# Sixteen instead of thirteen units of half-products in the first FFN, with fewer buffers for the adaLN pieces

## The chip, the cores and the metric

The kernel runs on one core of a Trainium2 chip. The metric is the device time of one execution in microseconds (us). PE is TensorE (matmuls; PEld its weight loads), DVE VectorE, ACT ScalarE, POOL GpSimd, SP SyncE, which issues nearly all DMAs; SPq is its DMA queue.

## The reference, cut to what matters

A two-layer trunk over 512 tokens of width 1024 in float32: a gated convolution mixer, an FFN, an SSD mixer, an FFN, each between two RMS norms and with shift, scale and gate from a conditioning vector c.

```python
mod = (jax.nn.silu(c) @ ada_w + ada_b).reshape(bsz, DEPTH, 2, 3, D_MODEL)
...
def swiglu_ffn(h, w_in, w_out):
    gate, up = jnp.split(h @ w_in, 2, axis=-1)
    return (jax.nn.silu(gate) * up) @ w_out
```

The change touches the FFN of the first layer: `h` is 512 x 1024, `w_in` 1024 x 5632 (2816 gate and 2816 up columns, 22 features of 128 columns each), `w_out` 2816 x 1024. `ada_w` is 1024 x 12288.

## The kernel before

Every float32 operand is split into a high half (a cast on ACT) and a low half (a subtraction on DVE); a product takes three matmuls for each 128 rows: high x high, high x low, low x high.

**In-projection.** A *chunk* (`in_chunk`, L318) is one feature's gate or up: 24 matmuls of 128x512. A *unit* (`Units`, from L612) makes two features' gate (even u) or up (odd u) at once, by seven half-products P1 to P7 of 12 matmuls of 128x256 each, from sums and differences of the weight's and the tokens' quarters: 84 small matmuls where two chunks take 48 large ones. Features 0 to 3 are chunks; then 13 units make features 4 to 15 and the gates of 16 and 17, and ten chunks make what is left. `UN1` (L1304) is the number of units.

**A unit's parts.** Unit u issues the DMAs for unit u + 2 (`fetch`): on SP the two sum quarters `sg` (L632, L633), then into the stage `wsu` the quarter [8:12] (L635), the two quarters of X, 512 KB, (L637) and the quarter [12:16] (L639); POOL then adds with two accumulating DMAs (L1403). PE runs P1(u), P7(u-1), P5(u), P2(u), P4(u-1), P6(u), P3(u). ACT casts X for u + 1 (L656), keeps results from the matmul banks (L704), casts Z, Y, S (L647); DVE makes the low halves (L660 for X, L648 for the others), combines results (c12 L712, c22 L721, c11 L708) and forms the sums Y and S (`sum_y` L673, `sum_s` L677). The banks of PE are few: P4(u-1) writes the bank from which c22(u-1) reads; P7(u-1) that from which ACT keeps A's high half.

**adaLN sums.** c's product with `ada_w` is made beside the units. A piece of `ada_w` (128 x 1024, 512 KB) is loaded into a tile `ada_st` (`ada_load`, L1040, its DMA at L1044), a *madd* on DVE (L128; L126 for the first of eight) adds it to `ada_acc`, and after eight a fold (L141) and a small matmul follow, whose results become `mods` (L152). Three pieces are loaded ahead; each madd is followed by the next `ada_load`. `sums(n)` (L1392) runs n such steps; it stands behind c11 in the units, one step in each even unit and in every one after the sixth. The tiles come from a pool of three buffers (L795).

**Order.** All engines follow the order in which the code is written. An instruction on SP that waits for a buffer holds up every later one on SP. Behind the units, the out-projection runs 28 products in seven groups (`seq`) and some plain ones, with its weights loaded by `x_load`, `xy_load`, `y_load`, and splits made ahead (`w_prep`, `a_prep`). Features up to 15 keep their raw product in `raw`; later ones are split at once.

```python
            for u in range(UN1):
                if not end:
                    un.fetch(u + 2)
                un.product(u, "P1")
                un.high_x(u + 1)
...
                un.c11(u)
                if u and (u % 2 == 0 or u > 6):
                    sums(1)
                un.split_z(u)
```

Of the kernel before, what the change touches and what calls it, by code (L numbers as in the profile page):

```python
# [16 lines left out]
P = 128  # L17
# [21 lines left out]
def trunk_kernel(  # L39
# [572 lines left out]
    class Units:  # L612
# [4 lines left out]
        def __init__(self, w1, h, tq, sums_w, s_tile, raw_at, gates, raw_done, count):  # L617
            self.w1, self.h, self.tq, self.sums_w = w1, h, tq, sums_w
            self.s_tile, self.raw_at, self.gates, self.raw_done, self.count = s_tile, raw_at, gates, raw_done, count
            self.staged, self.wts, self.banks, self.outs = {}, {}, {}, {}  # L620
# [6 lines left out]
        def fetch(self, u):  # L627
# [10 lines left out]
            if u:  # L638
                dma(st[:, 12:16, :], self.cols(u - 1, 1, 1))  # L639
# [28 lines left out]
        def split_s(self, u):  # L668
            self.split("S", u, self.s_tile(u), self.staged[u][0][:, 4:8, :])

# [121 lines left out]
    with ExitStack() as ph:  # L792
        sums_p, first_p = ExitStack(), ExitStack()
        gx = ph.enter_context(tc.tile_pool(name="gx", bufs=1, side="right", reuse_waits="tile"))
        ada_p.append(sums_p.enter_context(tc.tile_pool(name="adap", bufs=3, side="right", reuse_waits="tile")))  # L795
# [13 lines left out]

        def xn_tile():  # L810
# [11 lines left out]
        xf2s = ([ada_p[0].tile([P, 2, T], F32, tag="ada", name="xf") for _ in range(3)]  # L822
# [80 lines left out]
        with tc.manual_schedule(engines={PE_ENGINE, mybir.EngineType.SP, mybir.EngineType.Activation,  # L903
# [132 lines left out]

            def ada_tile():
                return ada_p[0].tile([P, 2, 512], F32, tag="ada", name="ada_st")
# [265 lines left out]
        UN1 = 13  # L1304
# [56 lines left out]

        def raw_done(f):
            if f % 4 == 3:
# [123 lines left out]
        def behind(q):  # L1487

            for t in range(2):
# [8 lines left out]
                elif q == at["s", 6 * per - 1]:  # L1498
                    held[1, 2 + t] = c22[:, t, :]
                    act.activation(c22[:, t, :], bank["A", t], AF.Copy, scale=-1.0)  # L1500
# [8 lines left out]
        with tc.manual_schedule(engines={PE_ENGINE, mybir.EngineType.SP, mybir.EngineType.Activation,  # L1509
                                         mybir.EngineType.DVE, mybir.EngineType.Pool}):  # L1510
            part_of = Units(f_w_in[0], h, tq, sums_w, s_tile, lambda f: raw[f // 4][:, f % 4, :], gates,
                            raw_done, UN1)
# [49 lines left out]
            un, fu, pp = part_of, 3 + UN1, UN1 + 1  # L1562
            for u in range(UN1):
                v = u - 1
                end = u == UN1 - 1
                if not end:
                    un.fetch(u + 2)
                else:
                    more_n = load_w([(f_w_in[0], DFF + (fu + 1) * P, P)], later=splits)
# [9 lines left out]
                un.keep(u, "A", 0, lo_)  # L1579
                un.product(u, "P5")  # L1580
# [10 lines left out]
                if u and (u % 2 == 0 or u > 6):  # L1591
                    sums(1)
# [7 lines left out]
                if end:  # L1600
                    for op in splits[2]:
                        op()
                else:
# [6 lines left out]
            load_pair(pp)  # L1610
            load_pair(pp + 1)
# [1305 lines left out]
```

## Time and profile before

| | us |
|---|---|
| median of three runs | 1306.29 (1306.22 to 1307.27) |
| the profiled execution | 1306.34 |
| its span | 1304.4 |
| granted TensorE clock, mean of the span | 0.998 |

The profile is of one execution. Its page gives busy times by engine, the chain of work that ended last, groups of instructions by line, and DMA issues with the time to landing. The trace behind it gives each instruction: a row of the timeline has its start, its length, the engine, the line, the operation, output <- input, and in brackets how long the engine stood idle before it and what ended that. A window's row has the busy time of each engine in a stretch, the granted clock, the DMA engines' share and the rate. A waits row has the engine that waited, whom it waited for, the total, the number and the longest. The units run from about 250 to 380 us, the ten chunks behind them to about 436, the out-projection behind those. PE's idle times in the units are no longer than 0.2 us.

### The profile page before, as it was taken

What the parts mean: (1) busy time and instruction counts of PE and PEld (TensorE: products, weight loads), DVE (VectorE), ACT (ScalarE), POOL (GpSimd) and SP (SyncE); (2) the same over time, 40 slices, a digit from 0 to 9 for tenths busy, and PEclk for the clock granted to TensorE, in tenths of its full rate; (3) what the DMA queues carried; (4) which work ended last, traced back from release to release, by engine and by line L of the source; (5) the groups of instructions that cost most, each with busy time, mean ns of one, the idle gap of its engine ahead of it and who ended that gap; (6) DMA issues with size and microseconds to landing.
All of it is one profiled execution on the core that took longest, in us unless ns stands there. A gap on an engine that the chain in (4) does not pass through costs nothing.

```text
span 1304.4 us, 20870 instructions
## 1 busy us (share of the span) xinstructions
PE 1292.9 (99%) x7949; PEld 1142.8 (88%) x7949; DVE 1055.9 (81%) x1617; ACT 744.3 (57%) x1321; POOL 133.8 (10%) x163
## 2 busy tenths in 40 slices
PE   8999999999999999999999999999999999999998
PEld 7788889999998888898888888888899999999886
DVE  5587898978877886758998999987878777778888
ACT  5423466455442566646765567755764555556666
POOL 0000011111100230000000000000100111110340
PEclk9999999999999999999999999999999999999999
DMA  9789661799977984437764457614532788888883
GB/s 309 229 260 294 189 194 50 202 238 239 241 212 261 250 151 123 140 122 222 226 215 152 140 189 218 186 49 150 157 98 59 197 216 211 199 203 271 214 159 90
DMA packets 230167, 245.37 MB, mean 188 GB/s; under 512 B 10788, under 2 KB 180660, under 8 KB 229044
## 3 DMA queue, kind: packets, MB, share of 16 engines
q1 hardware_dynamic: 206272, 194.31, 48.0%
q0 software_dynamic: 19648, 38.02, 16.0%
q10 hardware_dynamic: 4148, 11.73, 2.7%
q8 instruction: 62, 1.02, 0.3%
q14 instruction: 37, 0.30, 0.1%
HBM read 205.33 MB, written 4.34 MB: 161 GB/s over the span
## 4 chain that ended last, share of the span: by engine, by line
PE 93%; DVE 2%; DMA 2%; SPq 2%; ACT 1%; issue 0%; DVEq 0%; ACTq 0%
PE sA L694 14%; PE ip L305 10%; PE ip L307 9%; PE ip L306 9%; PE sC L694 7%; PE y L408 7%; PE cA L2630 5%; PE sB L694 3%; PE cA L1484 3%; PE li L305 3%; PE li L307 3%; PE li L306 3%; PE li L976 2%; PE y L1157 1%; PE y L2189 1%; PE cB L2630 1%
## 5 line engine op out<-in xcount | busy, mean ns | idle before, releaser
L305 PE MATMUL ip<-h,whl 128*128 128x512 f32 x592 | 234.1, 395 | 0.2 <-DVE cv L1076 0.2
L307 PE MATMUL ip<-h,whl 128*128 128x512 f32 x592 | 230.8, 390 | 0.0
L306 PE MATMUL ip<-h,whl 128*128 128x512 f32 x592 | 230.6, 390 | 0.0
L694 PE MATMUL sA<-tq,whl 128*128 128x256 f32 x1116 | 144.8, 283 | 0.0
L694 PEld LDWEIGHTS sA<-tq,whl 128*128 128x128 f32 x1116 | 138.7, 192 | 0.3 <-ACT g L704 0.2
L305 PEld LDWEIGHTS ip<-h,whl 128*128 128x128 f32 x592 | 111.2, 188 | 24.1 <-issue 1.8
L307 PEld LDWEIGHTS ip<-h,whl 128*128 128x128 f32 x592 | 111.2, 188 | 23.4
L306 PEld LDWEIGHTS ip<-h,whl 128*128 128x128 f32 x592 | 111.3, 188 | 22.2
L232 DVE TENSOR_TENSOR whl<-wst,whl 128x1024 fp32r<-128x1024 f32 x65 | 79.1, 1220 | 26.8 <-ACT whl L231 25.4
L128 DVE SCALAR_TENSOR_TENSOR ada_acc<-ada_st,csil,ada_acc 128x1024 f32<-128x1024 f32 x70 | 89.7, 1282 | 2.1 <-DMA ada_st<-in_ada_w_dram 0.8
L305 PE MATMUL li<-h,whl 128*128 128x256 f32 x288 | 83.5, 290 | 0.0
L307 PE MATMUL li<-h,whl 128*128 128x256 f32 x288 | 81.7, 284 | 0.0
L306 PE MATMUL li<-h,whl 128*128 128x256 f32 x288 | 81.6, 283 | 0.0
L231 ACT CAST whl<-wst 128x1024 fp32r<-128x1024 f32 x65 | 67.4, 1039 | 11.5 <-DMA wst<-in_a_w_in_dram 4.2
L408 PE MATMUL y<-whlo,ys 128*128 128x512 f32 x288 | 67.2, 392 | 0.0
L1860 DVE SCALAR_TENSOR_TENSOR cu<-ip,cols,cu 128x511 f32<-128x511 f32 (+2 forms) x84 | 62.8, 747 | 3.6 <-ACT cu L1857 1.4
L408 PEld LDWEIGHTS y<-whlo,ys 128*128 128x128 f32 x288 | 53.8, 188 | 11.4 <-issue 0.5
L2630 PE MATMUL cA<-whlo,ao 128*128 128x512 f32 x264 | 61.7, 391 | 0.0
L2630 PEld LDWEIGHTS cA<-whlo,ao 128*128 128x128 f32 x264 | 49.3, 188 | 11.2 <-DVE ao L2609 0.9
L647 ACT CAST whl<-sg 128x1024 fp32r<-128x1024 f32 x31 | 32.6, 1052 | 44.9 <-DVE sg L673 36.9
L305 PEld LDWEIGHTS li<-h,whl 128*128 128x128 f32 x288 | 55.3, 192 | 0.8 <-issue 0.8
L306 PEld LDWEIGHTS li<-h,whl 128*128 128x128 f32 x288 | 55.2, 192 | 0.0
(458 smaller groups left out, 2839.3 us busy)
## 6 DMA issues: line engine op xcount, KB each, us to landing
ada_st<-in_ada_w_dram SPq DMA_DIRECT2D x96, 512.0 KB, 6.5
wsu<-in_f_w_in_dram SPq DMA_DIRECT2D x32, 512.0 KB, 5.5
sg<-in_f_w_in_dram SPq DMA_DIRECT2D x62, 256.0 KB, 3.5
wsu<-in_f_w_in_dram SPq DMA_DIRECT2D x62, 256.0 KB, 4.6
wst<-in_m_w_in_dram SPq DMA_DIRECT2D x14, 1024.0 KB, 5.9
wst<-in_f_w_in_dram SPq DMA_DIRECT2D x10, 1024.0 KB, 5.1
wst<-in_m_w_in_dram SPq DMA_DIRECT2D x20, 512.0 KB, 5.4
wst<-in_a_w_in_dram SPq DMA_DIRECT2D x9, 1024.0 KB, 5.2
```

The costliest lines, as they stand in the source:

```text
L128: dve.scalar_tensor_tensor(acc, w, csil[:, k:k + 1], acc, MUL, ADD)
L231: later.append((lambda sw=sw, w=w: act.copy(w[:, 0, :nk, :], sw), lambda sw=sw, w=w: dve.tensor_tensor(w[:, 1, :nk, :], sw, w[:, 0, :nk, : ...
L232: lambda sw=sw, w=w: dve.tensor_tensor(w[:, 1, :nk, :], sw, w[:, 0, :nk, :].bitcast(F32), SUB)))
L305: pe.matmul(dst, w_at(w, 0, kk), a[:, 0, sl], start=start, stop=False)
L306: pe.matmul(dst, w_at(w, 0, kk), a[:, 1, sl], start=False, stop=False)
L307: pe.matmul(dst, w_at(w, 1, kk), a[:, 0, sl], start=False, stop=stop)
L408: pe.matmul(pst, a[:, al, tk], wt[:, wl, kk, :], start=i == 0 and k == (opens[hf][t] if opens else 0), stop=k == K - 1 and i == 2, skip_gr ...
L647: act.copy(dst[:, 0], src)
L694: pe.matmul(dst, w[:, wl, k0 + k, :], self.moving(q, k, al), skip_group_check=True, start=q in self.FIRST and k == 0 and i == 0, stop=k == ...
L1484: pe.matmul(bank[r, sub], a[:, al, q, tk], w[:, wl, q, :], start=first and k == 0, stop=False, skip_group_check=True)
L1860: dve.scalar_tensor_tensor(u[:, sft:], pst[:, :T - sft], w[3 - sft], u[:, sft:], MUL, ADD)
L2630: pe.matmul(bank[r][sub], a[:, al, q, tk], w[:, hl, q, :], start=first and k == 0, stop=last and k == 2, skip_group_check=True)
```

## The change

UN1 goes from 13 to 16: the units make features 4 to 19, and four chunks are left, gate and up of 20 and 21. The raw products of features 16 to 19 go into two tiles that are idle then (`raw4`: one of the pool `gx`, one called `got`), and are split behind products 10, 12, 14 and 16 of the out-projection (`raw_split`).

The pool of adaLN tiles goes from three buffers to two. Every third adaLN tile is `got`, until u is 9 (the list `few`); then `got` is needed for `raw4` and later for `c22`, and the pool's two buffers serve alone. Still three pieces are under way at a time. `sums` runs in every unit from the first on, with two steps in units 5, 8, 11 and 14; `sums(27)` behind the second leftover chunk runs what is left, and the out-projection's gate tile (`make_gg`) is made behind product 17.

The DMA at L639 goes for units above 1; ACT copies the same quarter from the sum tile instead (`twin`). The loads for the four chunks (`load_w`, `load_pair`) and for the out-projection (`x_load`, `xy_load`) are issued in the last unit and behind it, without `load_pair_at`.

The order of SP and DVE moves. First SP before the change, units 8 and 9 (L632 to L639 are a fetch of the unit's weights, L1044 loads an adaLN piece; the numbers tell tiles apart):

```order
L632 DMA sg_2233<-in_f_w_in_dram 128x4x128
L633 DMA sg_2233<-in_f_w_in_dram 128x4x128
L635 DMA wsu_3411<-in_f_w_in_dram 128x4x128
L637 DMA wsu_3411<-in_f_w_in_dram 128x8x128
L639 DMA wsu_3411<-in_f_w_in_dram 128x4x128
L1044 DMA ada_st_3494<-in_ada_w_dram 128x1024
...
L635 DMA wsu_3534<-in_f_w_in_dram 128x4x128
L637 DMA wsu_3534<-in_f_w_in_dram 128x8x128
L639 DMA wsu_3534<-in_f_w_in_dram 128x4x128
L1044 DMA ada_st_3619<-in_ada_w_dram 128x1024
```

SP after the change, units 8 to 10 (L1058 loads an adaLN piece):

```order
L1058 DMA ada_st_3516<-in_ada_w_dram 128x1024
L1058 DMA ada_st_3519<-in_ada_w_dram 128x1024
L632 DMA sg_2236<-in_f_w_in_dram 128x4x128
L633 DMA sg_2236<-in_f_w_in_dram 128x4x128
L635 DMA wsu_3559<-in_f_w_in_dram 128x4x128
L637 DMA wsu_3559<-in_f_w_in_dram 128x8x128
L1058 DMA ada_st_3644<-in_ada_w_dram 128x1024
...
L635 DMA wsu_3683<-in_f_w_in_dram 128x4x128
L637 DMA wsu_3683<-in_f_w_in_dram 128x8x128
L343 DMA gate_d_105<-gr_3766 8x128
L1058 DMA ada_st_3770<-in_ada_w_dram 128x1024
```

Five issues make a fetch before, four after. In both the adaLN load stands between two fetches. ada_st_3644 (unit 9) is the first that finds only two buffers: it takes that of ada_st_3516, whose madd stands in unit 10, and the fetch behind it on SP is unit 10's.

DVE after the change, unit 14, with two madds (L711 is c11, L648 low Z, L676 sum_y, L680 sum_s):

```order
L711 TENSOR_TENSOR g_4215<-sB_4233,g_4215 128x256
L152 TENSOR_TENSOR mods_98<-ada_ps_4139,cols2_92 32x8 x4
L128 SCALAR_TENSOR_TENSOR ada_acc_119<-ada_st_3894,csil_94,ada_acc_119 128x1024
L128 SCALAR_TENSOR_TENSOR ada_acc_119<-ada_st_4016,csil_94,ada_acc_119 128x1024
L648 TENSOR_TENSOR whl_4271<-wsu_4056,whl_4271 128x1024
L676 TENSOR_TENSOR sg_2236<-sg_2236,wsu_4056 128x512
L680 TENSOR_TENSOR wsu_4056<-sg_2236,wsu_4056 128x512
```

The second madd and the `mods` are what stands there between c11 and low Z beside the one madd that an earlier unit has. The last loads of the units on SP, after the change, in units 14 and 15:

```order
L1058 DMA ada_st_4142<-in_ada_w_dram 128x1024
L635 DMA wsu_4181<-in_f_w_in_dram 128x4x128
L637 DMA wsu_4181<-in_f_w_in_dram 128x8x128
L1058 DMA ada_st_4266<-in_ada_w_dram 128x1024
L1058 DMA ada_st_4269<-in_ada_w_dram 128x1024
L222 DMA wst_4309<-in_f_w_in_dram 128x8x128
L1436 DMA w2x_4312<-in_f_w_out_dram 128x512 x4
```

The load for the second leftover chunk (L222) stands behind two adaLN loads; before, one stood ahead of it.

The diff, cut to its core:

```diff
-            if u:
+            if u and not (self.twins and u > 1):
...
+        def twin(self, u):
+            act.copy(self.staged[u][0][:, 12:16, :], self.staged[u - 1][1][:, 1])
...
-        ada_p.append(sums_p.enter_context(tc.tile_pool(name="adap", bufs=3, side="right", reuse_waits="tile")))
+        gotp = ph.enter_context(tc.tile_pool(name="gotp", bufs=1, side="right", reuse_waits="tile"))
+        ada_p.append(sums_p.enter_context(tc.tile_pool(name="adap", bufs=2, side="right", reuse_waits="tile")))
...
+        def got_tile(name):
+            return gotp.tile([P, 2, T], F32, tag="got", name=name, bufs=1)
+
+        stage_of = []
+
+        def ada_tile(name="ada_st"):
+            stage_of.append(name)
+            if len(stage_of) % 3 == 0 and not few:
+                return got_tile(name)
+            return ada_p[0].tile([P, 2, T], F32, tag="ada", name=name)
+
+        raw4, few = [], []
...
-        UN1 = 13
+        UN1 = 16
...
+        def raw_at(f):
+            if f < NS:
+                return raw[f // 4][:, f % 4, :]
+            if f % 2 == 0:
+                raw4.append(gx.tile([P, 2, T], F32, tag="gg", name="raw4", bufs=1) if f == NS else got_tile("raw4"))
+            return raw4[f // 2 - NS // 2][:, f % 2, :]
+
+        def raw_split(f):
+            a, src = ff_tile(f), raw_at(f) if f % 2 else raw4[f // 2 - NS // 2][:, 0, :]
+            acts[f] = a
+            act.copy(a[:, 0, :], src)
+            dve.tensor_tensor(a[:, 1, :], src, a[:, 0, :].bitcast(F32), SUB)
...
                 end = u == UN1 - 1
+                if u == 9:
+                    few.append(u)
                 if not end:
                     un.fetch(u + 2)
                 else:
-                    more_n = load_w([(f_w_in[0], DFF + (fu + 1) * P, P)], later=splits)
+                    more_n = load_w([(f_w_in[0], (f0 + 1) * P, P)], later=splits)
+                    pair_tile("wxb", 1)
+                    wx.append(pair_x[0])
+                    for i in range(4):
+                        x_load(0, i)
...
+                if not end:
+                    un.twin(u + 2)
...
-                if u and (u % 2 == 0 or u > 6):
-                    sums(1)
+                if u:
+                    sums(2 if u % 3 == 2 and u > 2 else 1)
...
-            load_pair(pp)
-            load_pair(pp + 1)
             un.product(u, "P7")
             un.c12(u)
             tiles = [in_chunk(un.wts["X", UN1], h)]
             un.c22(u)
-            sums(2)
             for op in splits[3]:
                 op()
+            for step in todo:
+                next(step, None)
             un.product(u, "P4")
-            up(fu, tiles[0])
+            gate(f0, tiles[0])
             un.c21(u)
+            pair_tile("wxa", 2)
+            wx.extend(pair_x[1:])
+            for i in range(4):
+                x_load(1, i)
+            for p in (n_s - 2, n_s - 1):
+                xy_load(p)
+            for i in range(4):
+                x_load(2, i)
             tiles.append(in_chunk(more_n[0], h))
-            low_parts(1)
             for op in splits[4]:
                 op()
-            sums(2)
-            wx01 = sa.tile([P, 2, 2, 2, T], F32, tag="wxa", name="w2x")
-            wx += [wx01[:, 0], wx01[:, 1], sa.tile([P, 2, 2, T], F32, tag="wxb", name="w2x")]
             low_parts()
-            k0 = 4 + 2 * UN1
-            tiles = {k0 - 1: tiles[1]}
-            last = 2 * NF - 7
-            ws = {k0 + i: w for i, w in enumerate(ws[2:])}
-            splits = {k0 + i: op for i, op in enumerate(splits[3:])}
-            todo_w, todo_s = [], []
-
-            pair_st = {}
-
-            def load_pair_at(k, half):
-                if half == 0:
-                    st = pair_st[k] = wst_p.tile([P, 8, 256], F32, tag="wst", name="wst")
-                    for i in range(2):
-                        w = ws[k + i] = whl_p.tile([P, 2, 8, P], F32R, tag="whl", name="whl")
-                        src = st[:, :, i * P:(i + 1) * P]
-                        splits[k + i] = (lambda w=w, src=src: act.copy(w[:, 0], src),
-                                         lambda w=w, src=src: dve.tensor_tensor(w[:, 1], src,
-                                                                                w[:, 0].bitcast(F32), SUB))
-                c0 = (k - 2) // 2 % 2 * DFF + (4 + (k - 2) // 4 * 2) * P
-                dma(pair_st[k][:, 4 * half:4 * half + 4, :],
-                    f_w_in[0][half * T:(half + 1) * T, c0:c0 + 256].rearrange("(k p) f -> p k f", p=P))
-
-            for k in range(k0, last + 1):
-                if k - k % 2 + 4 <= last:
-                    load_pair_at(k - k % 2 + 4, k % 2)
-                if k < k0 + 6:
-                    for i in (0, 2):
-                        x_load((k - k0) % 3, i + (k - k0) // 3)
-                if k in (last - 2, last - 1):
-                    xy_load(n_s - 2 + k - last + 2)
-                tiles[k] = in_chunk(ws[k], h)
-                for step in todo:
-                    next(step, None)
-                q, j = divmod(k - 3, 4)
-                if j < 2:
-                    gate(4 + 2 * q + j, tiles[k - 1])
-                else:
-                    up(2 + 2 * q + j, tiles[k - 1])
-                for op in splits.get(k + 2, ()):
-                    op()
-                low_parts()
-                sums({last - 3: 2, last - 1: 2, last: 0}.get(k, 1))
-                if k == 2 * NF - 12:
-                    ggs.append(make_gg(1, gg_tile))
-                if k == last - 1:
-                    assert next(madds, 0) == 0 and not ada_sets and not quarters
-                    sums_p.close()
-                    ph.enter_context(tc.tile_pool(name="gap", bufs=1, side="right", reuse_waits="tile")).tile(
-                        [P, 216], F32, tag="gap", name="gap")
-                    ao_p.append(ph.enter_context(tc.tile_pool(name="aop", bufs=3, side="right", reuse_waits="tile")))
-                    ao_p[0].tile([P, 2, 2, 256], F32R, tag="ao", name="ao")
-                    gotp = ph.enter_context(tc.tile_pool(name="gotp", bufs=1, side="right", reuse_waits="tile"))
-                    c22 = gotp.tile([P, 2, T], F32, tag="c22", name="c22")
-                if k >= last - 1:
-                    w_prep(seq[k - last + 1])
-                    a_prep(seq[k - last + 1])
+            sums(27)
...
+                if q in (10, 12, 14, 16):
+                    raw_split(NS + q // 2 - 5)
+                if q == 17:
+                    ggs.append(make_gg(1, gg_tile))
```

More of the change, by code (lines that the diff above doesn't have):

```diff
@@ L615, in trunk_kernel, with __init__ @@
         FIRST = ("P1", "P5", "P2")
-        def __init__(self, w1, h, tq, sums_w, s_tile, raw_at, gates, raw_done, count):
-            self.w1, self.h, self.tq, self.sums_w = w1, h, tq, sums_w
+        def __init__(self, w1, h, tq, sums_w, s_tile, raw_at, gates, raw_done, count, twins=False):
+            self.w1, self.h, self.tq, self.sums_w, self.twins = w1, h, tq, sums_w, twins
             self.s_tile, self.raw_at, self.gates, self.raw_done, self.count = s_tile, raw_at, gates, raw_done, count
@@ L821, in trunk_kernel @@
         lead_src = {}
-        xf2s = ([ada_p[0].tile([P, 2, T], F32, tag="ada", name="xf") for _ in range(3)]
+        xf2s = ([ada_tile("xf") for _ in range(3)]
                 + [gx.tile([P, 2, T], F32, tag="gg", name="xf", bufs=1)])
@@ L1035, in ada_begin @@
                 return ada_steps()
-            def ada_tile():
-                return ada_p[0].tile([P, 2, 512], F32, tag="ada", name="ada_st")
             def ada_load():
@@ L1360, in a_ @@
             return v[:, :, int(name[2]) - 1, HALVES[int(name[1]) - 1]]
+        def raw_at(f):
[9 more added lines that the diff above has]
+            dve.tensor_tensor(a[:, 1, :], src, a[:, 0, :].bitcast(F32), SUB)
         def raw_done(f):
-            if f % 4 == 3:
+            if f < NS and f % 4 == 3:
                 p = f // 2 - 1
@@ L1498, in behind @@
                 elif q == at["s", 6 * per - 1]:
-                    held[1, 2 + t] = c22[:, t, :]
-                    act.activation(c22[:, t, :], bank["A", t], AF.Copy, scale=-1.0)
+                    if t == 0:
+                        c22.append(got_tile("c22"))
+                    held[1, 2 + t] = c22[0][:, t, :]
+                    act.activation(c22[0][:, t, :], bank["A", t], AF.Copy, scale=-1.0)
             for p in range(n_s):
@@ L1510, in trunk_kernel @@
                                          mybir.EngineType.DVE, mybir.EngineType.Pool}):
-            part_of = Units(f_w_in[0], h, tq, sums_w, s_tile, lambda f: raw[f // 4][:, f % 4, :], gates,
-                            raw_done, UN1)
+            part_of = Units(f_w_in[0], h, tq, sums_w, s_tile, raw_at, gates, raw_done, UN1, True)
+            c22 = []
             va = wst_p.tile([P, 4, T], F32, tag="wst", name="va")
@@ L1561, in trunk_kernel, with pair_tile @@
             plain_tiles = finish(())
-            un, fu, pp = part_of, 3 + UN1, UN1 + 1
+            un, f0 = part_of, 4 + UN1
+            pair_x = []
+            def pair_tile(tag, n):
+                t = sa.tile([P, 2 * n, 2, T], F32, tag=tag, name="w2x")
+                pair_x.extend(t[:, 2 * q:2 * q + 2] for q in range(n))
             for u in range(UN1):
@@ L1602, in trunk_kernel @@
                         op()
+                    load_pair(UN1 + 1)
                 else:
@@ new lines, in trunk_kernel @@
+            sums(27)
+            assert next(madds, 0) == 0 and not ada_sets and not quarters
+            sums_p.close()
+            ao_p.append(ph.enter_context(tc.tile_pool(name="aop", bufs=3, side="right", reuse_waits="tile")))
+            ao_p[0].tile([P, 2, 2, 256], F32R, tag="ao", name="ao")
+            w_prep(seq[0])
+            a_prep(seq[0])
+            gate(f0 + 1, tiles[1])
+            tiles.append(in_chunk(ws[2], h))
+            for step in todo:
+                next(step, None)
@@ L1686, in trunk_kernel @@
+            w_prep(seq[1])
+            a_prep(seq[1])
+            up(f0, tiles[2])
+            low_parts()
+            tiles.append(in_chunk(ws[3], h))
+            last = 3
             w_prep(seq[2])
```

## The prediction

> **What bounds the kernel now.** First the page's span, its busy times and its chain that ended last, by engine.
>
> ```profile
> span 1304.4 us, 20870 instructions
> PE 1292.9 (99%) x7949; PEld 1142.8 (88%) x7949; DVE 1055.9 (81%) x1617; ACT 744.3 (57%) x1321; POOL 133.8 (10%) x163
> PE 93%; DVE 2%; DMA 2%; SPq 2%; ACT 1%; issue 0%; DVEq 0%; ACTq 0%
> ```
>
> PE is busy all the time and is nearly the whole chain. So the time falls only where PE gets less work, and it rises with any wait that reaches PE. Next the windows of two units (10, and an earlier one; each from a unit's third product to that of the next).
>
> ```profile
> core 0: us, PE busy (x) PEld busy (x) DVE busy (x) ACT busy (x) POOL busy (x), PEclk, DMA share, GB/s
> 351.28:361.56 10.28, 10.28 (x86) 10.12 (x85) 9.35 (x17) 4.60 (x7) 1.73 (x2) 1.00 1.00 258
> 310.74:320.82 10.08, 10.08 (x86) 10.08 (x85) 8.97 (x14) 4.73 (x8) 1.77 (x2) 1.00 0.98 249
> ```
>
> The second row is a plain unit: seven products in 10.08 us, and DVE at 8.97 of them. The first (unit 10) holds a stall of 0.20, below. The granted clock is 1.00, and the DMA engines are full (share 0.98 and 1.00). Such a unit has little slack on DVE and on DMA. Now the timeline of units 9 and 10.
>
> ```profile
> 338.10 1.60 PE L694 MATMUL sA<-h,whl 128*128 128x256 f32 x12
> 339.51 0.37 SPq L632 DMA_DIRECT2D sg<-in_f_w_in_dram  x1
> 339.54 1.60 PE L694 MATMUL sA<-tq,whl 128*128 128x256 f32 x12
> 339.93 0.50 SPq L633 DMA_DIRECT2D sg<-in_f_w_in_dram  x1
> 341.22 0.37 SPq L635 DMA_DIRECT2D wsu<-in_f_w_in_dram  x1
> 341.64 0.50 SPq L637 DMA_DIRECT2D wsu<-in_f_w_in_dram  x1
> 344.13 0.42 DVE L708 TENSOR_TENSOR raw<-sB,raw 128x256 f32<-128x256 f32 x1 [1.65 <-PE sB L694]
> 344.47 1.27 DVE L128 SCALAR_TENSOR_TENSOR ada_acc<-ada_st,csil,ada_acc 128x1024 f32<-128x1024 f32 x1
> 345.78 0.34 SPq L1044 DMA_DIRECT2D ada_st<-in_ada_w_dram  x1
> 348.39 1.60 PE L694 MATMUL sA<-h,whl 128*128 128x256 f32 x12
> 349.30 1.05 ACT L656 CAST whl<-wsu 128x1024 fp32r<-128x1024 f32 x1
> 351.45 1.22 DVE L660 TENSOR_TENSOR whl<-wsu,whl 128x1024 fp32r<-128x1024 f32 x1
> 352.59 0.42 DVE L721 SCALAR_TENSOR_TENSOR raw<-sA,raw 128x256 f32<-128x256 f32 x1
> 352.92 0.38 ACT L704 COPY g<-sC 128x256 f32<-128x256 f32 x1 [2.29 <-PE sC L694]
> 354.16 3.04 PE L694 MATMUL sA<-tq,whl 128*128 128x256 f32 x24
> 356.95 0.88 POOL L1403 DMA_DIRECT2D wsu<-wsu  x1 [0.69 <-DVE ada_acc L128]
> ...
> 380.38 0.40 PE L305 MATMUL ip<-h,whl 128*128 128x512 f32 x1
> 385.84 1.60 PE L694 MATMUL sA<-tq,whl 128*128 128x256 f32 x12
> ```
>
> P1 of unit 9 starts at 338.10, P7 of unit 8 at 339.54: a product is 1.44 us, a unit 7 x 1.44 = 10.08. The last two rows bracket a chunk: 5.46 us. On SP the fetch for unit 11 goes out 1.4 us (L632) to 3.5 us (L637) after P1. The adaLN load goes out at 345.78, 0.04 us after the madd that frees its buffer (344.47 + 1.27). Call the end of a unit's (last) adaLN madd F: in unit 9 it lies 7.64 us after P1. P4 of unit 9 starts 354.16 - 348.39 = 5.77 after P1 of unit 10; it overwrites the bank that c22 (L721) reads, so it needs c22, which stands on DVE behind the low half of X (L660).
>
> **The work that goes.** Three more units are 30.24 us; the six chunks they replace are 32.76. PE gains **-2.48**. The adaLN matmuls and the out-projection's products stay as many.
>
> **The wait that comes.** From unit 9 on two buffers carry the adaLN pieces with two still to be summed, so a load needs the *next* unit's madd, and SP keeps its order: fetch(12) to fetch(16) and the loads behind them stand behind that wait. Before, a load waited for the madd just made, and SP bore that at no cost:
>
> ```profile
> SPq L1044 <- DVE ada_acc L128: 42.8, 14, 8.7
> ```
>
> (total, times, longest, 250 to 440 us.) In unit 10 fetch(12) thus starts at F instead of 1.4 us after P1. The bytes of X(12) come from L637:
>
> ```profile
> L637 SPq DMA_DIRECT2D wsu<-in_f_w_in_dram x32: 446/505/510, 231.9 to 1162.6; - x32
> DMA to landing us min/median/max: 4.6/5.5/6.5
> ...
> L637 SPq DMA_DIRECT2D wsu<-in_f_w_in_dram x12: 499/500/510, 253.6 to 363.5; - x12
> DMA to landing us min/median/max: 4.6/4.9/5.8
> ```
>
> Landing is 4.6/4.9/5.8 in this stage and 4.6/5.5/6.5 over the run. The late fetch goes out together with an adaLN load, so I take 5.5 and keep 4.6 and 6.5. The other durations:
>
> ```profile
> L342 DVE COPY gr<-ggp 8x128 f32<-8x128 f32 x1 | 0.3, 271 | 0.0
> L141 DVE TRANSPOSE_TENSOR_REDUCE fold<-ada_acc 128x32 f32<-128x1024 f32 x3 | 3.7, 1242 | 0.1
> L126 DVE TENSOR_SCALAR ada_acc<-ada_st,csil 128x1024 f32<-128x1024 f32 x2 | 1.6, 820 | 0.0
> L1365 DVE TENSOR_TENSOR s1t<-raw 128x512 f32<-128x512 f32 x4 | 2.7, 684 | 0.0
> L647 ACT CAST wss<-wsu 128x512 fp32r<-128x512 f32 x12 | 7.5, 623 | 0.0
> 354.77 0.68 DVE L152 TENSOR_TENSOR mods<-ada_ps,cols 32x8 f32<-32x8 f32 x4
> 359.61 0.36 ACT L704 COPY g<-sA 128x256 f32<-128x256 f32 x1
> 360.03 1.49 PEld L694 LDWEIGHTS sA<-tq,whl 128*128 128x128 f32 x12 [0.16 <-ACT g L704]
> 372.87 0.37 SPq L222 DMA_DIRECT2D wst<-in_f_w_in_dram  x1
> 376.73 1.05 ACT L231 CAST whl<-wst 128x1024 fp32r<-128x1024 f32 x1 [0.18 <-DMA wst<-in_f_w_in_dram]
> ```
>
> Let T be P1 of unit 10. F(10) = 7.64 + 0.20 (the gate rows' copy, L342, partly overlapped) = T+7.84. From F to P4: adaLN load, two sg quarters, L635 and gaps to L637's issue 1.80; landing 5.5; cast 1.10; low X 1.26; c22 0.34; PE 0.06: P4(10) at F + 10.06 = T+17.90. It is due at T + 10.08 + 5.77 = T+15.85. PE loses **2.06** in unit 11.
>
> From there on it is a loop. c11 (0.34) and the next madd (1.20) follow c22, the load follows the madd, the fetch follows the load. Its period is 10.00 + 0.34 + 1.20 = 11.54 against PE's 10.08. Unit 11 has a fold (1.24) and a first piece (0.82) for its madd: F(11) = T+20.27. F(12) = 31.81. Unit 13 has a low part in addition (0.60, L1365): F(13) = 43.95. Unit 14 another and the small mods (0.66): F(14) = 56.75, counted to its first madd, which frees the load. The fetch in unit 15 has no sg quarters (-0.97): P4(14) at T+65.84, due at 15.84 + 4 x 10.08 = 56.16. PE is **9.68** late there, the first 2.06 included. Last, the load of the second leftover chunk (L222) waits for F(15) = 65.84 + 0.34 + 1.20 - 0.06 = 67.32, goes out at 67.73, lands in 3.8 (372.87 to the cast's start, 376.73 less 0.06) and is cast (1.13); keep A hi (0.33) stands behind that cast on ACT, and P7(15) needs its bank: 73.0 against 9.68 + 50.40 + 10.08 = 70.16, **+2.8**. All of it: **+12.5** in units 11 to 15.
>
> I take these ends: nothing (case b below); with 4.6 for the five landings -4.5; with 6.5 +5, and with 5.2 for the chunk's load +1.4 more.
>
> **Doubled sums.** DVE's order is madd, low Z, sum_y; then Y hi and keep A hi on ACT; then P7 on PE. In unit 10 of before the mods (0.68) and a column put that chain 0.79 later, and PE lost 0.20 (10.28 against 10.08; the row of 360.03 names keep A hi). Slack is 0.59, say 0.56. Unit 5 has 0.85 in addition (0.82 and a gap): +0.3. Unit 8 has a madd more, 1.31: +0.75. Together **+1.05**. Doubles in 11 and 14 lie beside the late fetch. Bounds: 0 and 2.2.
>
> **What costs nothing.** The 14 copies on ACT take about 0.63 each (623 ns, the cast of the same shape); ACT is busy 4.7 of 10 us, and each copy has a unit until its reader. It may wait for POOL's second sum of the fetch before (issued at 356.95, 1.5 us ahead of the next P1); behind it on ACT stands keep C hi, 4.5 us after P1 (352.92 - 348.39). So the sum has 6 us to land unnoticed, and each us past that would cost PE one; I take 0. One of the fetch's five transfers goes; what that gains lies within the lower landing. In the out-projection four splits join DVE's work:
>
> ```profile
> 469.41:480.29 10.88, 10.88 (x49) 9.01 (x48) 9.99 (x18) 7.14 (x13) 3.96 (x5) 1.00 1.05 219
> ```
>
> DVE there goes from 9.99 to at most 11.35 of 10.88 (0.68 for the low part every second product, two products to this window). Weights are prepared several products ahead, so it takes that up: 0, at most 0.5. In the tail after unit 15 the loads go out 8 to 15 us ahead of their readers: 0.
>
> The sum: 1306.34 (the profiled execution; its span is 1304.4 and about 2 us lie around it; the median is 1306.29, the same within 0.05) - 2.48 + 1.05 + 12.5 = **1317.4 us**.
>
> One rule of the skill beside this: the Trainium skill, "TensorE: Matmul & The Clock Gate", Part 1, says that the TensorE clock falls to half after an idle window of about 3.4 us and returns after a busy one. My longest stall is 2.8 us, so by that rule the clock stays; an estimate from the page's window: a stall above 3.4 us would add about 1.7 us. Every row quoted here has 1.00, so no run here shows it.
>
> **The rivals.**
> (a) The forecast, 1312 to 1324 by the landings: **0.72**. For it: order and buffers make the wait, and both DMA and DVE are near full.
> (b) No block: the late load finds its buffer free, because the sums run a piece ahead of what I count or the third buffer still serves. Then the doubles decide: -2.48 + 0.3 + 0.75 + 0.33 (unit 11: a fold and a first piece) + 1.41 (unit 14: mods and a madd) = +0.3, 1306.6; were the doubles hidden too, 1303.9. It decides where the way from F to c22 falls under 8.0 us (10.00 less the 2.06 of the first stall), that is at a landing of 3.4 us. Against it: the shortest landing of 32 is 4.6. **0.12**.
> (c) The block bites in part only: landings near 4.6 and a loop that keeps up after the first stalls, 1306 to 1312: **0.10**.
> (d) The POOL chain comes on top: fetch, POOL's sum, copy, keep C, low Z, sum_y, Y hi, keep A hi, P7. By the rows it has about the loop's period and lies nearly hidden behind it; a slow sum or a lower clock makes 1324 to 1330: **0.06**.
>
> **How the numbers follow.** The likeliest is (a), 1317.4. The range 1308 to 1324 leaves out (b), a part of (c) and (d), together 0.2. A run can tell 0.2% or 2.6 us from no change: faster is under 1303.7, slower above 1308.9. Faster: the hidden doubles of (b), 0.05. Same: the rest of (b) and the lower half of (c), 0.12. Slower: 0.83.
>
> **What would show it.** SP's queue waits for DVE's ada_acc at L1058 in units 10 to 15; L632 to L637 go out some 8 us after P1 there; ACT's L656 waits for the DMA into wsu; PE stands before P4, released by c22 (L724); units come every 11.5 to 12.8 us from 11 on and every 10.1 before; ACT's cast of wst holds the last P7 up. Units at 10.1 throughout would refute the loop. A stall before P7 by keep A hi instead of before P4 by c22 would mean (d). Chunks and the out-projection unchanged in length would show that the rest costs nothing.

## The result and the profile after

The changed kernel takes 1329.60 us (median of five runs, 1328.26 to 1331.72) against 1306.22: ratio 1.0182, 95% interval 1.0167 to 1.0196. The forecast was 1317.4 us, with a range of 1308 to 1324. The sign was right, the forecast rise of 11.1 us was half of the 23.4 that came, and the time lies outside the range.

The profiled execution took 1331.72 us. Its page, the same lines as those shown of before:

```profile
span 1329.6 us, 21136 instructions
PE 1302.0 (98%) x8057; PEld 1153.3 (87%) x8057; DVE 1068.4 (80%) x1638; ACT 759.7 (57%) x1354; POOL 138.8 (10%) x169
PE 87%; DMA 5%; DVE 3%; SPq 2%; ACT 2%; issue 1%; POOL 0%; DVEq 0%; POOLq 0%; ACTq 0%
```

PE's share of the chain fell from 93 to 87%, and DMA's rose from 2 to 5%: PE now waits for loads. And PE is busy for 9 us longer although it has 2.5 us less to do, so that some of its work ran slower. Next come the windows of the whole stage, from the first product of unit 0 to the first of the out-projection, of before and then of after. They place the loss:

```profile
250.27:436.66 186.39, 186.39 (x1341) 176.80 (x1339) 146.67 (x196) 88.44 (x142) 20.25 (x24) 1.00 0.87 239
```

```profile
251.21:459.49 208.28, 193.10 (x1448) 186.88 (x1447) 158.53 (x215) 101.60 (x171) 25.44 (x29) 0.96 0.79 208
```

The stage is 21.9 us longer. 15.2 of its 208.28 us are idle on PE, and the mean granted clock is 0.96 where it was 1.00. Of the other 3.3 us of the span's difference of 25.2, the out-projection has 2.5 (110.2 before, 112.7 after), and 0.9 stands ahead of the stage (the first product of unit 0 starts between 249.9 and 251.6 us in the profiles of all the runs, of either kernel); behind the out-projection the two kernels agree within 0.3.

The timeline of unit 11, whose P1 starts at 360.64 and that of unit 10 at 350.56:

```profile
358.42 0.34 SPq L1058 DMA_DIRECT2D ada_st<-in_ada_w_dram  x1
358.86 1.30 SPq L632 DMA_DIRECT2D sg<-in_f_w_in_dram  x1
360.21 0.50 SPq L633 DMA_DIRECT2D sg<-in_f_w_in_dram  x1
360.82 0.45 SPq L635 DMA_DIRECT2D wsu<-in_f_w_in_dram  x1
361.32 0.65 SPq L637 DMA_DIRECT2D wsu<-in_f_w_in_dram  x1
367.74 1.04 ACT L656 CAST whl<-wsu 128x1024 fp32r<-128x1024 f32 x1 [5.74 <-DMA wsu<-in_f_w_in_dram]
368.81 1.23 DVE L660 TENSOR_TENSOR whl<-wsu,whl 128x1024 fp32r<-128x1024 f32 x1 [5.28 <-ACT whl L656]
369.96 0.42 DVE L724 SCALAR_TENSOR_TENSOR g<-sA,g 128x256 f32<-128x256 f32 x1
370.43 5.49 PE L697 MATMUL sA<-tq,whl 128*128 128x256 f32 x24 [3.87 <-DVE g L724]
```

Read it from the top. The adaLN load leaves at 358.42, 0.03 us after the end of unit 10's madd, and the fetch of unit 12 stands behind it: X of unit 12 is asked for at 361.32. The cast of X waits 5.74 us for it, c22 (L724) stands behind the low half, and P4 starts 3.87 us late. This is the forecast's chain, link by link. The last row has the second thing to see: P4 and P6 take 5.49 us for the 24 matmuls that took 3.04 before. The windows of 10 us of the stage's second half show why:

```profile
core 0: us, PE busy (x) PEld busy (x) DVE busy (x) ACT busy (x) POOL busy (x), PEclk, DMA share, GB/s
350.00:360.00 10.00, 10.00 (x86) 10.00 (x85) 8.83 (x13) 5.29 (x9) 0.00 (x0) 1.00 0.31 52
360.00:370.00 10.00, 6.56 (x55) 6.35 (x53) 4.68 (x8) 3.67 (x6) 1.73 (x2) 0.98 0.86 222
370.00:380.00 10.00, 9.57 (x58) 9.57 (x59) 7.98 (x12) 4.45 (x8) 1.00 (x2) 0.68 0.70 187
...
410.00:420.00 10.00, 10.00 (x72) 10.00 (x72) 9.09 (x15) 4.06 (x7) 0.88 (x1) 0.83 0.63 187
...
430.00:440.00 10.00, 8.23 (x30) 7.07 (x31) 3.90 (x5) 2.37 (x3) 0.00 (x0) 0.66 1.03 362
```

From 350 to 360 the DMA engines move 52 GB/s, since SP is held; then PE idles; and in the window behind each long idle time the granted clock (the column behind POOL's) is 0.68, 0.83 or 0.66. The waits of PE in the stage and of SP from 340 to 430, and the landing of the fetches there:

```profile
PE sA L697 <- DVE g L724: 7.0, 3, 3.9
PE sA L697 <- ACT raw L707: 3.8, 1, 3.8
PE sA L697 <- DVE raw L724: 3.0, 1, 3.0
...
SPq L1058 <- DVE ada_acc L128: 51.2, 5, 12.1
...
L637 SPq DMA_DIRECT2D wsu<-in_f_w_in_dram x6: 497/498/652, 345.7 to 413.6; - x6
DMA to landing us min/median/max: 4.6/6.3/7.0
```

PE waits for c22 (L724) before P4 and once for keep A hi (L707) before the last P7, as forecast. The fetches land in 6.3 us (the median), not in 5.5. The out-projection's groups, of before and of after, are the third thing:

```profile
L1484 PE MATMUL cA<-whlo,ao 128*128 128x512 f32 x192 | 44.3, 390 | 0.0
```

```profile
L1511 PE MATMUL cA<-whlo,ao 128*128 128x512 f32 x192 | 45.7, 397 | 0.0
```

The same 192 matmuls take 397 ns instead of 390, without any idle time, at a clock of 1.00. From start to start they stand 234.3 ns apart instead of 226.7 (mean over the trace's starts).

### The profile page after: what moved, and what is told of

Same layout as the page of the kernel before. It is cut to its first block, busy times and chain, and to the rows that moved or that the text cites. A ratio compares the mean times of both kernels' runs of the same rounds, so it can differ in the third digit from the quotient of the medians.

```text
span 1329.6 us, 21136 instructions
## 1 busy us (share of the span) xinstructions
PE 1302.0 (98%) x8057; PEld 1153.3 (87%) x8057; DVE 1068.4 (80%) x1638; ACT 759.7 (57%) x1354; POOL 138.8 (10%) x169
## 3 DMA queue, kind: packets, MB, share of 16 engines
q8 instruction: 63, 1.03, 0.3%
## 4 chain that ended last, share of the span: by engine, by line
PE 87%; DMA 5%; DVE 3%; SPq 2%; ACT 2%; issue 1%; POOL 0%; DVEq 0%; POOLq 0%; ACTq 0%
PE sA L697 11%; PE ip L305 10%; PE ip L307 9%; PE ip L306 9%; PE y L408 7%; PE sC L697 5%; PE cA L2642 5%; PE cA L1511 3%; PE sB L697 3%; PE li L305 3%; PE li L307 3%; PE li L306 3%; DMA wsu<-in_f_w_in_dram 3%; DMA wsu<-wsu 2%; PE li L993 1%; PE y L1171 1%
## 5 line engine op out<-in xcount | busy, mean ns | idle before, releaser
L305 PE MATMUL ip<-h,whl 128*128 128x512 f32 x544 | 215.8, 397 | 0.2 <-DVE cv L1090 0.2
L306 PE MATMUL ip<-h,whl 128*128 128x512 f32 x544 | 212.5, 391 | 0.0
L307 PE MATMUL ip<-h,whl 128*128 128x512 f32 x544 | 212.4, 390 | 0.0
L697 PE MATMUL sA<-tq,whl 128*128 128x256 f32 x1224 | 164.8, 290 | 15.2 <-DVE g L724 7.0
L697 PEld LDWEIGHTS sA<-tq,whl 128*128 128x128 f32 x1224 | 156.9, 198 | 17.3 <-DVE g L724 7.7
L305 PEld LDWEIGHTS ip<-h,whl 128*128 128x128 f32 x544 | 102.6, 189 | 22.4 <-issue 1.8
L307 PEld LDWEIGHTS ip<-h,whl 128*128 128x128 f32 x544 | 102.5, 188 | 21.9
L306 PEld LDWEIGHTS ip<-h,whl 128*128 128x128 f32 x544 | 102.6, 189 | 20.6
L647 ACT CAST whl<-sg 128x1024 fp32r<-128x1024 f32 x34 | 35.8, 1052 | 54.6 <-DVE sg L676 46.0
L1430 POOL DMA_DIRECT2D sg<-sg x34 | 29.8, 876 | 308.7 <-DMA sg<-in_f_w_in_dram 185.4
L660 DVE TENSOR_TENSOR whl<-wsu,whl 128x1024 fp32r<-128x1024 f32 x35 | 42.7, 1219 | 17.1 <-ACT whl L656 17.1
```

The source lines that it names most:

```text
L305: pe.matmul(dst, w_at(w, 0, kk), a[:, 0, sl], start=start, stop=False)
L306: pe.matmul(dst, w_at(w, 0, kk), a[:, 1, sl], start=False, stop=False)
L307: pe.matmul(dst, w_at(w, 1, kk), a[:, 0, sl], start=False, stop=stop)
L660: dve.tensor_tensor(dst[:, 1], self.staged[u][0][:, 0:8, :], dst[:, 0].bitcast(F32), SUB)
L697: pe.matmul(dst, w[:, wl, k0 + k, :], self.moving(q, k, al), skip_group_check=True, start=q in self.FIRST and k == 0 and i == 0, stop=k == ...
```

## The experiments

The theory (T): the wait of the adaLN load for the next unit's madd, ahead of the fetches on SP, makes the stalls. Its rivals: the copies on ACT and the chain through POOL; the sixteen units themselves, with their doubled sums. Two more questions came with the profile: whether the clock falls because PE idles and what that costs, and what slows the out-projection's matmuls. All times are medians beside runs of the kernel before on the same chip (1306.0 to 1306.6).

### e1_lag: two pieces under way

```diff
                     ada_madd(ada_acc, st.rearrange("p a b -> p (a b)"), k)
-                    ada_load()
+                    if few == [9]:
+                        few.append(0)
+                    else:
+                        ada_load()
```

> After, but from unit 9 on two adaLN pieces are under way instead of three (one load is left out there, so that each later one waits for the madd just made). If SP's wait for the next unit's madd is the cause of the loss, the fetches go out 1.4 to 3.5 us after P1 in all units, PE has no stall before P4 and the granted clock stays 1.00: 1306.2 - 2.5 + 1.1 (doubles up to unit 8) + 1.7 (doubles in 11 and 14) + 2.5 (slower matmuls of the out-projection) = 1309, between 1306 and 1311. If instead the chain through POOL and the copies on ACT is the cause, units stay longer than 11 us and the time stays above 1320.

Measured: 1310.63 us, ratio 1.0031 (1.0021 to 1.0040), near the 1309 of T and 19 us less than with the change as it was. The waits of SP from 340 to 430 and of PE in the units, and the window that had no DMA traffic in the profile of after:

```profile
SPq L1058 <- DVE ada_acc L128: 9.1, 6, 2.6
...
PE sA L697 <- ACT g L707: 1.6, 2, 1.2
...
350.00:360.00 10.00, 10.00 (x86) 10.00 (x85) 8.97 (x13) 5.03 (x10) 2.18 (x3) 1.00 1.02 222
```

SP's wait fell from 51.2 to 9.1 us, no P4 waits any longer, and DMA runs at 222 GB/s where it ran at 52. T holds: one load less under way, and nothing else, takes 19 of the 23 us away. The two waits left (0.4 and 1.2 us) are the doubled sums.

### e2_gap and e6_before_nogap: where the tiles ao lie

The compiled programs place `ao` at 211328 before (a multiple of 128 bytes) and at 208096 after (32 beyond a multiple of 64): the change drops a tile `gap` of 864 bytes ahead of that pool. e2 puts 32 bytes there, in the changed kernel. In e2, e6 and e7 below, the other operand of these matmuls, `whlo`, keeps its addresses in the built program:

```diff
             sums_p.close()
+            ph.enter_context(tc.tile_pool(name="gap", bufs=1, side="right", reuse_waits="tile")).tile(
+                [P, 8], F32, tag="gap", name="gap")
```

> After, with 32 bytes left free ahead of the tiles ao, so that their addresses are multiples of 64 bytes as before. If the address makes the out-projection's matmuls slower (237.6 against 230.1 ns from start to start, 336 of them), these come back to 230 ns and the time falls by 2.5 us to 1327. If the slowdown comes from the added splits or the DMAs beside it, nothing changes (1329.6).

Measured: 1330.07 us, no change, and a miss. The matmuls stand 233.3 ns apart. (The expectation has 237.6 and 230.1 ns where the trace's starts give 234.3 and 226.7; the difference is the same.) An address at a multiple of 64 bytes brings 1 of the 7.5 ns. So the other direction was tried, in the kernel before:

```diff
-                    ph.enter_context(tc.tile_pool(name="gap", bufs=1, side="right", reuse_waits="tile")).tile(
-                        [P, 216], F32, tag="gap", name="gap")
```

> Before without the 864 bytes left free ahead of the tiles ao: their addresses move from multiples of 128 bytes to 32 bytes beyond one of 64, as in the changed kernel. If the address sets the spacing of the matmuls that load from them, it goes from 226.7 to 234.3 ns in the seven groups of the out-projection, 336 matmuls, and the time rises by 2.5 us to 1309. If it was the splits added there, it stays at 1306.5.

Measured: 1308.72 us, ratio 1.0020 (1.0011 to 1.0029), with the spacing at 234.3 ns. The row of the same group is that of after, in a kernel that has none of its splits:

```profile
L1484 PE MATMUL cA<-whlo,ao 128*128 128x512 f32 x192 | 45.7, 397 | 0.0
```

The out-projection is as long as that of after, 112.7 us. The address alone makes the 2.5 us.

### e3_busy and e11_busy2: PE kept busy in the stalls

e3 computes P2 of a unit once more, into the same bank with the same values, where PE would idle; e11 does it twice:

```diff
                 un.product(u, "P2")
+                for _ in range(2 * (u > 10)):
+                    un.again(u, "P2")
...
+            for _ in range(2):
+                un.again(u, "P2")
             un.product(u, "P7")
```

(e3: once each instead of the two loops.)

> After, with P2 of units 11 to 15 computed twice into the same bank, and that of unit 15 a third time ahead of P7: 1.44 us more of PE work in each of the long stalls, with no result changed. If a long idle time of PE lowers the granted clock, the stalls of 3.0 to 3.9 us shrink to 1.6 to 2.4, the clock stays at 1.00, and the time falls by the 3 us that the last drop costs, to about 1326.6; the drops in between cost little, since the loop through SP sets the start of the next P4. If the drops in between add up, it falls by some 8 us, to 1321. If idle time does not lower the clock, the drops stay and the time is 1329.6 or more.

Measured: 1330.46 us, a miss: not lower. Its stalls before P4 of unit 10 and before the last P7 are 2.85 and 2.44 us, and behind them the windows still have 0.84 and 0.83: an idle time of 2.4 us lowered the clock too. The test therefore didn't separate its theories, and more work was put into the stalls:

> After, with P2 of units 11 to 15 computed three times in place, and that of unit 15 twice more ahead of the last P7 (2.9 us of PE work in each long stall instead of 1.44). If idle time of PE lowers the granted clock, nothing is left of the drops: 1.00 in every window, and from P7 of the last unit to the out-projection 24.7 us instead of 27.7; the time falls by up to 3 us where the loop through SP sets the start of P4, and rises where the extra work outlasts a stall (units 12 and 14, up to 1.5 us each). If the drops have another cause, they stay.

Measured: 1329.88 us. The same windows as above:

```profile
350.00:360.00 10.00, 10.00 (x86) 10.00 (x85) 9.19 (x14) 5.13 (x9) 0.00 (x0) 1.00 0.29 63
360.00:370.00 10.00, 9.23 (x77) 9.03 (x76) 4.94 (x8) 3.22 (x7) 1.73 (x2) 1.00 0.80 202
370.00:380.00 10.00, 10.00 (x85) 9.98 (x84) 6.86 (x9) 4.28 (x9) 1.72 (x2) 1.00 0.77 200
...
410.00:420.00 10.00, 8.75 (x74) 8.55 (x73) 8.82 (x15) 4.47 (x8) 0.88 (x1) 1.00 0.66 196
...
430.00:440.00 10.00, 8.54 (x49) 7.39 (x49) 3.10 (x5) 2.37 (x3) 0.00 (x0) 1.00 1.03 352
```

The clock is 1.00 in all of them, with the longest idle time 1.46 us. So it is PE's idle time that lowers it. From the last P7 to the out-projection it is 24.9 us instead of 27.7: there the drop costs 2.8 us. In the units it costs nothing: the last P7 starts 182.7 us after the first P1 here, and 180.6 in the changed kernel, whose clock had fallen twice by then. In that kernel's trace the P4 behind each of these two drops still has to wait for c22, 0.13 us at 383.52 and 1.63 us at 423.35. The loop through SP sets when P4 can start, and a slower P4 only fills the next wait. That is also why 17.3 us of additional PE work (12 products of 1.44) cost only 2.1 us in the units; with the 2.8 won behind them the time stays as it was.

How long an idle time must be shows when the windows are laid on the steps of the granted clock. In this stage the half clock lasts for one or two steps of 3.41 us, which lie on one grid in each trace. First the changed kernel around its last P7, then a stretch of e5_before_two (below):

```profile
427.65:431.07 3.42, 0.28 (x3) 0.07 (x1) 0.00 (x0) 0.67 (x1) 0.00 (x0) 1.00 0.96 286
431.07:434.48 3.41, 2.71 (x12) 2.72 (x13) 2.25 (x3) 0.64 (x2) 0.00 (x0) 0.50 1.05 380
434.48:437.89 3.41, 3.41 (x9) 2.65 (x9) 0.42 (x1) 0.85 (x1) 0.00 (x0) 0.50 1.08 372
437.89:441.31 3.42, 3.42 (x16) 2.81 (x15) 1.23 (x1) 0.20 (x1) 0.00 (x0) 1.00 0.95 352
```

```profile
367.25:370.66 3.41, 1.89 (x16) 1.69 (x15) 0.00 (x0) 0.93 (x1) 1.73 (x2) 1.00 0.95 200
370.66:374.08 3.42, 1.66 (x13) 1.66 (x14) 3.10 (x5) 2.54 (x6) 0.00 (x0) 1.00 0.45 78
374.08:377.49 3.41, 3.41 (x31) 3.41 (x30) 2.94 (x4) 1.91 (x4) 0.00 (x0) 1.00 0.73 205
```

In the first, PE idles for 3.14 us of one step, and the clock is 0.50 in the next two. In the second, a single idle time of 3.28 us (369.14 to 372.42) is divided between two steps, with 1.52 and 1.76 us, and the clock stays at 1.00. In this stage, over all the runs, each of the 14 drops follows a step with 1.96 us or more of idle PE, and no step with 1.76 or less is followed by one. So what counted is the idle part of a step, and not the length of the idle time.

### e4_notwin: the quarter loaded again

```diff
-            part_of = Units(f_w_in[0], h, tq, sums_w, s_tile, raw_at, gates, raw_done, UN1, True)
+            part_of = Units(f_w_in[0], h, tq, sums_w, s_tile, raw_at, gates, raw_done, UN1)
...
-                if not end:
-                    un.twin(u + 2)
```

> After, with the quarter loaded by a fifth DMA of each fetch as before, and no copies on ACT. If the block on SP is the cause, the DMA only adds to it: 256 KB more behind each late fetch, 1330 to 1334. If the copies on ACT (and their wait for POOL's sums) are a cause, the time falls by 5 us or more.

Measured: 1334.08 us, 4.5 more than with the copies. The rival falls: the copies help. It is not the late fetches that grow, though. In the trace the last P7 starts 182.9 us after the first P1, 2.3 later than in the changed kernel, and these 2.3 us are there before the late fetches reach PE: P7 waits for keep A hi 2.12 us at 353.71, where it doesn't wait with the copies, and 0.77 for 0.43 us in the unit before.

### e5_before_two: the wait alone, in thirteen units

```diff
+        gotp3 = sums_p.enter_context(tc.tile_pool(name="gotp3", bufs=1, side="right", reuse_waits="tile"))
-        ada_p.append(sums_p.enter_context(tc.tile_pool(name="adap", bufs=3, side="right", reuse_waits="tile")))
+        ada_p.append(sums_p.enter_context(tc.tile_pool(name="adap", bufs=2, side="right", reuse_waits="tile")))
...
+            if len(stage_of) % 3 == 0 and not few:
+                return gotp3.tile([P, 2, T], F32, tag="got", name=name, bufs=1)
...
+                if u == 7:
+                    few.append(u)
```

> Before (13 units, ten chunks, no copies, no doubles) with one piece of the change alone: from unit 7 on two buffers carry the adaLN pieces with three under way, so that from unit 8 on a load waits for the next unit's madd, ahead of the fetches of units 9 to 11 and of the second chunk's load. If that wait makes the loss, PE stalls 3.9 us before P4 in unit 10, some 2.7 us in each of units 11 and 12, about 3 us before the last P7, and loses about 3 us to the granted clock: 1306.5 + 12 to 15, so 1318 to 1322. If the loss needs the sixteen units or the copies, the time stays between 1306 and 1309.

Measured: 1337.46 us, ratio 1.0237 (1.0222 to 1.0251): in kind as T said, and twice the size. The stalls in the units are 3.5, 3.3, 0.7 and 3.75 us, near what was expected. What the expectation left out is that this kernel has ten chunks behind its units, and the same wait goes on there:

```profile
398.08 21.20 SPq L1050 DMA_DIRECT2D ada_st<-in_ada_w_dram  x3
...
PE ip L305 <- ACT whl L1653: 4.9, 1, 4.9
ACT whl L1653 <- DMA wst<-in_f_w_in_dram: 15.3, 2, 8.5
```

(A row of SP's timeline, and the waits from 330 to 480.) Three adaLN loads hold SP from 398 to 419; the weight loads of the later chunks (L1657) stand behind these and the adaLN loads that follow, their casts on ACT (L1653) wait 15.3 us for them, and PE idles 4.9 us at 441.9 before a chunk. The clock falls for five steps of 3.41 us, which cost PE some 7 us by their busy part, and the out-projection takes 115.7 us instead of 110.2. The wait needs neither sixteen units nor the copies.

### e7_lag128, e8_late: both mends, and the doubled sums moved

e7 is e1 with `gap` as in e2, but `[P, 24]`, 96 bytes, which puts `ao` at 208000, a multiple of 128.

> After with two adaLN pieces under way from unit 9 on, and 96 bytes left free ahead of the tiles ao, so that they stand at multiples of 128 bytes (64 alone gave 233.3 ns instead of 234.3). If 128 bytes is what counts, the spacing is 226.7 ns and the time is 1310.6 - 2.5 = 1308. If not, 1310.6.

Measured: 1308.19 us, ratio 1.0013 (1.0004 to 1.0022), spacing 226.7 ns. 128 bytes is what counts. Then the second step of the doubled sums was moved to the unit's end:

```diff
-                    sums(2 if u % 3 == 2 and u > 2 else 1)
+                    sums(1)
...
                 if not end:
                     un.split_s(u + 1)
+                if u % 3 == 2 and u > 2:
+                    sums(1)
```

> The kernel of the run before in this list (lag and 128 bytes), with the second adaLN step of units 5, 8, 11 and 14 moved behind the splits of S, so that the sums for Y don't wait for it. If the doubles cost by that chain (0.4 us in 5, 0.4 in 9, 1.15 in 14), they cost nearly nothing now: 1308 - 1.7 = 1306.4, at or a little under the kernel before. If DVE as a whole is too full in these units, it stays at 1308 or above.

Measured: 1308.84 us: a miss, nothing gained. The stall of 1.16 us before the P7 in unit 15 is gone, but one of 1.03 before the P7 in unit 14, again behind keep A hi, and three of 0.2 to 0.3 came in its place.

### e9_keep, e10_best, e12_before_keep: the order on ACT

e9 is e7 with the copy of A's high half ahead of Y's cast, so that P7 doesn't wait for the sums:

```diff
                 if u:
                     un.c21(v)
+                un.keep(u, "A", 0, hi_)
...
                 un.product(u, "P3")
-                un.keep(u, "A", 0, hi_)
```

> The kernel with two adaLN pieces under way and 128-byte addresses (1308.2), with ACT's copy of A's high half (keep A hi) ahead of the cast of Y instead of behind it: P7 then no longer waits for the chain low Z, sum_y, Y. If the doubled sums cost by that chain, the stalls before P7 (0.4 us in unit 9, part of 0.37 in 6, and 1.15 in 15) go or shrink to 0.6, and the time falls by 1 to 1.8 us to 1306.4 to 1307.2. If they cost by DVE's load, P5 waits instead and it stays at 1308.

Measured: 1305.80 us, ratio 0.9998 (0.9989 to 1.0007), 2.4 us less than e7 and more than was expected; in the trace the stage is 1.6 us shorter, as expected. So it is for the most part the chain that costs, not DVE's sum of work. One stall of 0.58 us is left in the units, before P5 behind a low half (L648), in the one behind the double and the small mods. e10 takes that as well:

```diff
-                    sums(2 if u % 3 == 2 and u > 2 else 1)
+                    sums(2 if u in (5, 8, 11) else 1)
...
             un.c22(u)
+            sums(1)
             for op in splits[3]:
```

> The run before this one, and the second adaLN step of unit 14 moved behind the last unit, where DVE stands idle for 5 us. Nothing that stalls PE for more than 0.3 us is left, so the 2.5 us of less PE work show, less about 1 us of small matmuls and short stalls: 1305 to 1306, at or a little below the kernel before (1306.4). If DVE's load still decides, 1307 to 1308.

Measured: 1304.48 us, ratio 0.9987 (0.9978 to 0.9996): the fastest of all, 1.7 us below the kernel before. No idle time over 0.15 us is left on PE in the stage, whose window is

```profile
250.02:433.88 183.86, 183.86 (x1449) 180.00 (x1447) 157.70 (x215) 103.39 (x171) 25.17 (x29) 1.00 0.90 235
```

183.86 against 186.39 us before: 2.53 less, the saved PE work of the forecast. Whether that comes from the units or from the order on ACT, the last run tells, which has that order in the kernel before:

> Before (13 units) with keep A hi ahead of the cast of Y, as in the two runs before. If the gain of the best kernel (1304.5 against 1306.2) comes from the sixteen units, this one gains only the two short stalls of before, 0.2 us each: 1305.8. If it comes from the earlier copy, this one reaches 1304.5 as well.

Measured: 1306.29 us, ratio 1.0000 (0.9991 to 1.0009). The gain is that of the units.

## Why the prediction was right in kind and wrong in size

**The work that goes: right.** -2.48 forecast (its two figures, 32.76 and 30.24, differ by 2.52), -2.53 in e10.

**The doubled sums: right.** +1.05 forecast up to unit 10; from the first P1 to that of unit 10 it is 99.35 us after and 98.12 before, +1.2. With the block gone (e1) the stalls of units 9 and 15 are at the place that was named, before P7 behind keep A hi, with 0.43 and 1.15 us (1.41 was the sum for unit 14's double).

**The wait: right in its mechanism, mis-sized by 8 us.** F(10) was to be at T+7.84 and is at T+7.83. The step that failed is the next one, "P4(10) at F + 10.06": it is at F + 12.04. Its terms were 1.80 from F to L637's issue, measured 2.93 (the first sg quarter's issue took 1.30 us for 0.37), and 5.5 to its landing, measured 6.4. Round the loop the five issues cost 3.5 us more than I had, and the five landings (6.39, 6.15, 6.47, 5.23, 6.99) 3.7; the second chunk's load landed in 5.0 instead of 3.8. The last P7 was forecast 73.0 us after T and came 81.2 after it. I had taken 5.5 between ends of 4.6 and 6.5, from transfers that start with SP free. A fetch that was held goes out in one burst behind another 512 KB, with the sg quarters ahead of X, so that row was not a fair sample for it; its upper end, the fetch at 231.9 us, which goes out with adaLN loads around it, was the nearest. That the burst is what lengthens landings and issues is argued, and no run changes it alone. The longer landings by themselves (3.7 and 1.2 us) would have made 1322.3, inside the range. The issues, the clock and the addresses, for which the forecast had no bounds or a bound of 0.5, took the time out of it.

**The clock: set aside by a number that was too small.** "My longest stall is 2.8 us, so by that rule the clock stays" failed with the stalls: they are 3.87, 3.04 and 3.84, and the clock fell with each of them. It cost 2.8 us behind the last unit (e11) and nothing in the units. The rule, the Trainium skill, "TensorE: Matmul & The Clock Gate", Part 1, has an idle window of about 3.4 us, free-running. In direction these runs agree with it, and their steps are 3.41 us long on one grid. In size they differ, and the measurement decides: idle times of 2.44 and 2.85 us (e3) lowered the clock too, and 1.96 us in one step (e4) was enough, while one of 3.28 us over two steps (e5) didn't. So even a stall of the forecast's 2.8 us could have lowered it. The forecast's estimate of 1.7 us fits a drop of one step (26.5 us from the last P7 to the out-projection in e3 and e4, for 24.8 in e1); the changed kernel had two. A stall near the bound should have been carried as a term of its own, with the price of the stage behind it.

**The out-projection: a term that was missing.** "So it takes that up: 0, at most 0.5" was right for the four splits: with them (after) and without them (e6) the out-projection takes 112.7 us at these addresses. But the removal of the tile `gap`, which stands in the diff, was passed over. It costs 2.5 us, by addresses.

**The rest.** 8.2 us from the loop, 2.8 from the clock and 2.5 from the addresses, with 0.2 from the units ahead of it, make 13.7 of the 14.3 us between the forecast and the profiled execution (1331.7); 0.9 us more stood ahead of the stage in that execution, within what its start varies by from run to run, and 0.3 less behind the out-projection. Of the rivals, (b) was the mechanism that e1 made true by hand: without the block +4.1, of which 2.5 is addresses; the stage alone is 0.2 us longer than before (186.59), and (b) had +0.3. Rival (d), the POOL chain, did not show: no stall before P7 in units 11 to 14 was longer than 0.7 us.

## What to carry to other kernels

When buffers are cut, cut the loads under way by as many: a load that waits for a buffer holds up everything behind it in its queue, and its price is a loop (wait, issue, landing, casts, next wait) in which each duration is the one of a burst, not the median of a free queue. A stall of PE is worth more than its length where nothing behind it can hide the lower clock, and no more than its length where the next wait hides it; look at what sets the next start. And an address is part of a change: a tile that seems to hold nothing may be there for the alignment of the next pool.

## What the runs showed of the hardware that was not expected

The spacing of 128x512 matmuls depends on where the 128x128 fp32r weight tile lies: 226.7 ns at multiples of 128 bytes (before, e7), 233.3 at 64 beyond (e2), 234.3 at 32 beyond a multiple of 64 (after, e6), at a granted clock of 1.00, with LDWEIGHTS shown as 188 ns in all of them and with the moving operand at the same addresses in each pair of kernels that differ in this alone. Why an offset of the stationary operand shows in the spacing was not tried.

The granted clock is halved in steps of 3.41 us, and by the idle part of one step: 1.96 us or more of idle PE in a step was followed by 0.50, 1.76 or less by 1.00, so that a single idle time of 3.28 us passed without a drop and one of 2.44 didn't. A step at 0.50 was followed by a second when PE idled for 0.70 us or more of it, and by 1.00 at 0.56 or less. How the idle part is measured on the chip is not shown. PE could be kept at 1.00 by repeating a product into its own bank, at no cost in time (e11, 1329.88 us for 1329.60).
